# Two planes for the experts' rows, one engine for the normalised rows, and attention three items ahead

## The chip, the core and the metric

One core of a Trainium2 chip runs the whole program in one launch. Its engines are TensorE (PE, with PEld for the loading of its weights), VectorE (DVE), ScalarE (ACT), GpSimd (POOL) and SyncE (SP, which only issues DMAs here). The metric is the device time in microseconds; each time below is a median of several runs, beside one execution that was profiled.

## What is computed

Two blocks over 1024 tokens of width 1024, in float32. The first normalises, mixes (gated linear attention and causal pooling), adds, and then sends each token through two of 32 experts. The second has a short convolution and a dilated window attention, and adds again.

```python
def hier_moe(h, ...):                       # block 1, second half
    g_p, g_idx = lax.top_k(jax.nn.softmax(g_logits, axis=-1), 1)      # 1 of 4 groups
    e_top, e_idx = lax.top_k(e_logits, TOP_K_IN_GROUP)                # 2 of its 8 experts
    gate = g_p * jax.nn.softmax(e_top, axis=-1)
    ...                                     # rows sorted by expert, padded
    def expert_block(args):
        xb, e = args
        return (jax.nn.silu(xb @ w_gate[e]) * (xb @ w_up[e])) @ w_down[e]
    y_rows = y_rows * row_w[:, None]
    out = jnp.zeros((T + 1, D)).at[row_token].add(y_rows)[:T]

def first_block(x, ...):
    ...
    h2 = rmsnorm(x, norm2_g[l])
    x = x + hier_moe(h2, ...)
    return rmsnorm(x, norm_f_g)

def second_block(x, ...):
    h = rmsnorm_2(x, norm_w)
    u, g_b, g_c, z_conv, q, k, v, z_attn = jnp.split(h @ w_in, splits, axis=-1)
    y_conv = short_gated_conv(u, g_b, g_c, conv_w, conv_b) * jax.nn.silu(z_conv)
    for window, dilation in ((128, 1), (512, 4), (2048, 16)):
        o_i, lse_i = dilated_window_attention(q, k, v, rel_bias, window, dilation)
    o = softmax(lses) weighted sum of the o_i
    y = jnp.concatenate([y_conv, o * jax.nn.silu(z_attn)], axis=-1)
    return x + y @ w_out
```

## The kernel before

The tokens are eight tiles of 128 rows. Each float32 product is made of three matmuls: `split` (L124 to L131) casts an operand to its high part on ScalarE and subtracts that on VectorE for the low part (both stand as L127), and `mm3` (L160 to L163) multiplies high by high, high by low and low by high. Large tiles share a pool of slots named `blk`; an allocation waits for the last reader of the slot. Each engine and each DMA queue runs its instructions in one fixed order. SP's queue (q1 in the rows) carries the weights; POOL's queue (q0) carries the gathers, the scatters and some writes. A helper `late` holds closures back by a number of steps and so sets where small pieces of work stand between the matmuls.

**The router's end.** As a tile of block 1's first half is done, `route_rows` (L523) writes its x1 to the DRAM tensor `x_acc`, transposes it and splits it (`turn`), makes the router's logits and at last its normalised row h2, which goes to the DRAM tensor `h_rows`. Tiles 0 to 6 make h2 on VectorE (L568); tile 7 makes it with two multiplies on POOL (L531, L532), written by SP (L968). After the eighth tile `route_half`, `places` and `slots` give every token its row among its two experts' rows, by matmuls of one-hot tables (`val`, L653, and L664), and `row_tables` (L671 to L677) turns the sums into `row_idx`, the token of each of 96 rows of each expert, and `row_wgt`.

**The experts.** For each of 32 experts `gather_rows` (L980) fetches 96 rows of `h_rows` into one of four buffers `xg`, four experts ahead; `load_expert` (L270 to L285) loads six pieces of 512 KB of weights five experts ahead, a load waiting for the fifth before it; the rows are transposed, multiplied, and `down` scales the result into `yt` (L1045, ScalarE). `add_rows` (L985, POOL's queue) adds `yt` into `x_acc` by a scatter that accumulates. Unused rows have an index out of bounds and are skipped. The last expert's rows are added for tokens 0 to 511 by a matmul with one-hot `picks` straight into block 2's input (`add_last`, L1068 to L1076), since block 2 starts with them, and scattered too for the rest. A loop (`For_i`, L1128) for rows beyond 96 of an expert follows; here it runs no time, but every engine reads its bound behind its earlier work.

**Block 2's inputs.** After the loop `load_cols` (L308) loads x2 of tokens 0 to 511 as `x2c`, four loads of 512 KB. TensorE transposes them, and VectorE and ScalarE make the operands `g` (L129, L130). Tokens 512 to 1023 are loaded later by `load_x2` (L1219), while the products of the convolution run.

**The attention.** Four pairs of heads times twelve items (three dilations, four parts) make a stream of 48 items. For each, `load_values` loads `vt` from `v_rows` (three slots), `powers` multiplies queries and keys (L1500), takes a minimum on VectorE (L1506) and an exponential on ScalarE (L1508, into `sb`), `turn_powers` transposes `sb` (L1526) and copies it (L1528, L1530), and `weigh` multiplies with `vt` (L1559). The loop of L1684 runs `powers` two items ahead, `turn_powers` one ahead. `by_class` (L1480 to L1489) copies a pair's queries and keys into the order of a dilation, on POOL (L1487). `deliver` (L1655) loads partial sums `xs` by POOL's queue.

Of the kernel before, what the change touches and what calls it, by code (L numbers as in the profile page):

```python
# [20 lines left out]
P = 128  # L21
# [44 lines left out]
def first_then_second_block(ctx: ExitStack, tc: tile.TileContext, a: dict, out: bass.AP):  # L66
# [413 lines left out]
    row_idx = C.tile([P, NE], I32, name="row_idx")  # L480
    row_wgt = C.tile([P, NE], F32, name="row_wgt")
# [38 lines left out]
    last_h2 = []  # L520

    def route_rows(t, x1):
        ss = S.tile([P, 1], F32, name="ss1", tag="ss1", bufs=4)  # L523
        sq = blk("sq", (P, D))
        A.activation(sq, x1, AF.Square, accum_out=ss)
        r = mean_rstd(ss, 1, D)
        if t < NT - 1:
            G.dma_start(x_acc[t * P:(t + 1) * P], x1)  # L528
        else:
            h2 = blk("h2", (P, D))  # L530
            G.tensor_mul(h2, x1, r.to_broadcast([P, D]))  # L531
            G.tensor_mul(h2, h2, g2)  # L532
            G.dma_start(x_acc[t * P:(t + 1) * P], x1)
            last_h2.append(h2)
# [24 lines left out]

        def folded(lt):  # L560
            lp = psum((P, 36))
            PE.matmul(lp, lt, fold, start=True, stop=True)
            V.scalar_tensor_tensor(lgs[t // 4][:, t % 4, :], lp, r, br, op0=OP.mult, op1=OP.add)
            if t % 4 == 3:
                route_half(t // 4)
            if t < NT - 1:
# [21 lines left out]
    def route_half(hf):  # L588
# [26 lines left out]
        val = blk("val", (P, 4, 2, 5, NE), BF16)  # L615
        A.activation(val[:, :, :, 0, :], oh[:, ts], AF.Copy, scale=pcol)
        for i in range(4):
            A.activation(val[:, i, :, 1, :], oh[:, 4 * hf + i], AF.Copy, scale=float(4 * hf + i + 1))
        late.at(1 if hf else PLACES, lambda: places(hf, val, gp, e1, e2))

    def places(hf, val, gp, e1, e2):
# [31 lines left out]
        V.tensor_mul(val.rearrange("p t k v e -> p (t k) v e")[:, :, 2:, :],  # L653
# [4 lines left out]
    def slots(hf, val, sels):  # L658
        if hf == 0:
            slot_ps.append(psum((P, 5, NE)))  # L660
# [7 lines left out]
    def row_tables(idx, w, ps, n, pool):  # L668
        f = pool.tile([P, n], F32, name="ri_f", tag=f"rif{n}", bufs=1)
        e = pool.tile([P, n], F32, name="ri_e", tag=f"rie{n}", bufs=1)  # L670
        sv = pool.tile([P, 5, n], F32, name="ri_s", tag=f"ris{n}", bufs=1)  # L671
# [3 lines left out]
        V.scalar_tensor_tensor(idx, f, -float(P), e, op0=OP.add, op1=OP.add)  # L675
        V.tensor_add(e, sv[:, 2, :], sv[:, 3, :])
# [3 lines left out]
    def half(hf):  # L680
# [28 lines left out]
        if hf == 0:  # L709
            behind(lambda: w_q.extend(w_q0()))  # L710
        else:
            w_q += pair(w_in, 0)
        if hf == 0:
# [254 lines left out]
    SY.dma_start(h2_d[(NT - 1) * P:], last_h2[0])  # L968
    load_expert(3)
    late.flush()  # L970
    row_tables(row_idx, row_wgt, slot_ps[0], NE, R)
# [63 lines left out]
    def down(e):  # L1035
# [10 lines left out]
        if e < NE - 1:  # L1046
            add_rows(yt, row_idx[:, e:e + 1], CAP)
# [9 lines left out]
    last_idx = S.tile([P, 1], I32, name="last_idx", bufs=1)  # L1057
    picks = blk("picks", (P, 512), F32R)

    def place_last():  # L1060
        at = S.tile([P, 5], F32, name="last_at", bufs=1)
        V.tensor_copy(last_idx, row_idx[:, NE - 1:NE])
        V.tensor_copy(at[:, 4:], last_idx)
        for i in range(4):
            V.tensor_scalar(at[:, i:i + 1], at[:, 4:], float(-P * i), None, op0=OP.add)
            V.tensor_scalar(picks[:, i * P:(i + 1) * P], iota_s, at[:, i:i + 1], None, op0=OP.is_equal)

    def add_last(c):  # L1068
        for j in range(2):
            ps = psum((P, 2, 256))  # L1070
            for i in range(2):
                b = 2 * j + i
                for part in range(2):
                    PE.matmul(ps[:, i, :], picks[:CAP, b * P:(b + 1) * P], last_y[1 + part][:CAP, 256 * c:256 * c + 256],
# [51 lines left out]

    end_reg = nc.values_load(n_more[0:1, 0:1], min_val=0, max_val=NOB)
    with tc.For_i(0, end_reg, 1):  # L1128
# [24 lines left out]
        rv = E.tile([P, NT, 2, 5], BF16, name="rv")  # L1153
# [5 lines left out]
        sp = psum((P, 5))  # L1159
# [7 lines left out]
        row_tables(li, lw, sp.rearrange("p (a b) -> p a b", b=1), 1, E)  # L1167
# [36 lines left out]
        add_rows(lyt, li, P)  # L1204
# [10 lines left out]
    def load_x2():  # L1215
        xs = []
        for t in range(4, NT):
            xt = blk(f"x2_{t}", (P, D))
            SY.dma_start(xt, x_acc[t * P:(t + 1) * P])  # L1219
            xs.append(xt)  # L1220
# [52 lines left out]
    yc = [blk("yc0", (P, T))] + [W.tile([P, T], F32, name=f"yc{j}") for j in range(1, 4)]  # L1273
# [3 lines left out]
    qT = [blk(f"qT{j}", (P, T)) for j in range(4)]  # L1277
    for j in range(4):
        V.memset(qT[j][:, 0:1], 0.0)
        V.memset(kT[j][:, 0:1], 0.0)  # L1280
# [5 lines left out]
    def conv(hf, cc):  # L1286
# [35 lines left out]
        def convolve(m):  # L1322
            ct, u = 2 * cc + m, us[m]
            cv = yc[ct]
# [85 lines left out]
    for f in c0[:4] + c1[:4] + c0[4:] + c1[4:] + attn_gate(0):  # L1410
        f()
    x2 = load_x2()
# [167 lines left out]
    def mix_weights(hp):  # L1580
# [16 lines left out]
        def spread():  # L1597
            ps = psum((48, P))
            PE.transpose(ps, sw.rearrange("p c h b -> p (c h b)"), ident)
            swT = W.tile([48, P], F32, name="swT", tag="swT", bufs=1)  # L1600
# [84 lines left out]
    for g in range(-2, NS):  # L1685
        if g + 2 < NS:
            hp, cfg, pr = stream[g + 2]
            if g == -2:
# [89 lines left out]
```

## Time and profile before

| | us |
|---|---|
| median of 3 runs | 1626.17 (1624.89 to 1628.64) |
| the profiled execution | 1627.21 |
| its span (first to last instruction) | 1625.5 |
| busy in it: TensorE, VectorE, ScalarE, POOL | 1535.9, 1021.1, 801.2, 210.8 |

TensorE's mean granted clock is 0.972 of full speed. The experts take the stretch from about 640 to 985, the attention that from 1345 to 1570. Read busy times by stretch, not for the whole span; a stretch in which TensorE is busy throughout at clock 1.00 has nothing to gain from other engines. A wait names what came last before an instruction could start.

### The profile page before, as it was taken

What the parts mean: (1) busy time and instruction counts of PE and PEld (TensorE: products, weight loads), DVE (VectorE), ACT (ScalarE), POOL (GpSimd) and SP (SyncE); (2) the same over time, 40 slices, a digit from 0 to 9 for tenths busy, and PEclk for the clock granted to TensorE, in tenths of its full rate; (3) what the DMA queues carried; (4) which work ended last, traced back from release to release, by engine and by line L of the source; (5) the groups of instructions that cost most, each with busy time, mean ns of one, the idle gap of its engine ahead of it and who ended that gap; (6) DMA issues with size and microseconds to landing.
All of it is one profiled execution on the core that took longest, in us unless ns stands there. A gap on an engine that the chain in (4) does not pass through costs nothing. (4 is left out here: it accounts for less than half of the span.)

```text
span 1625.5 us, 24026 instructions
## 1 busy us (share of the span) xinstructions
PE 1535.9 (94%) x8678; PEld 1266.6 (78%) x8678; DVE 1021.1 (63%) x2278; ACT 801.2 (49%) x1635; POOL 210.8 (13%) x196
## 2 busy tenths in 40 slices
PE   7999999999999994999989897999999999999899
PEld 6888888887888874998888786888877787666667
DVE  5596444667644355998877686766655545676663
ACT  4434323453433232888777684524443326866550
POOL 1000000000000003232232111200000100243311
PEclk9999999999999996999999998999999999999999
DMA  6233334436323458999999996434423331445445
GB/s 193 65 82 106 103 109 163 136 115 195 104 80 115 142 215 281 295 270 319 328 312 335 296 335 194 156 102 164 149 88 104 104 103 41 120 119 147 103 137 169
DMA packets 168022, 272.01 MB, mean 167 GB/s; under 512 B 32689, under 2 KB 111932, under 8 KB 167773
## 3 DMA queue, kind: packets, MB, share of 16 engines
q1 hardware_dynamic: 154204, 232.13, 44.5%
q0 software_dynamic: 13680, 38.32, 8.5%
q8 instruction: 69, 1.13, 0.3%
q14 instruction: 53, 0.43, 0.1%
q10 hardware_dynamic: 16, 0.00, 0.0%
HBM read 243.92 MB, written 39.59 MB: 174 GB/s over the span
## 5 line engine op out<-in xcount | busy, mean ns | idle before, releaser
L127 ACT CAST wh<-wr 128x512 fp32r<-128x512 f32 (+1 forms) x248 | 170.6, 716 | 341.9 <-PE ps L162 192.5
L127 DVE TENSOR_TENSOR wl<-wr,wh 128x512 fp32r<-128x512 f32 (+1 forms) x248 | 202.3, 832 | 169.4 <-ACT wh L127 162.7
L127 DVE TENSOR_TENSOR wl<-ew,wh 128x1024 fp32r<-128x1024 f32 x144 | 172.6, 1220 | 44.3 <-ACT wh L127 43.6
L161 PE MATMUL ps<-h,wh 128*128 128x512 f32 x448 | 176.8, 395 | 0.0
L127 ACT CAST wh<-ew 128x1024 fp32r<-128x1024 f32 x144 | 149.7, 1052 | 54.4 <-PE ps L163 34.8
L163 PE MATMUL ps<-h,wl 128*128 128x512 f32 x448 | 175.3, 391 | 0.0
L162 PE MATMUL ps<-h,wh 128*128 128x512 f32 x448 | 175.3, 391 | 0.0
L161 PE MATMUL ps<-g,wh 128*128 128x512 f32 x320 | 126.1, 395 | 0.0
L162 PE MATMUL ps<-g,wh 128*128 128x512 f32 x320 | 125.2, 392 | 0.0
L163 PE MATMUL ps<-g,wl 128*128 128x512 f32 x320 | 124.8, 391 | 0.0
L161 PE MATMUL ps<-wh,xh 128*96 128x256 f32 x384 | 112.3, 293 | 6.2 <-ACT act L1023 6.2
L162 PE MATMUL ps<-wl,xh 128*96 128x256 f32 x384 | 110.9, 289 | 1.5 <-DVE wl L127 1.5
L163 PE MATMUL ps<-wh,xh 128*96 128x256 f32 x384 | 110.8, 289 | 0.0
L163 PEld LDWEIGHTS ps<-h,wl 128*128 128x128 f32 x448 | 84.6, 189 | 17.8
L161 PEld LDWEIGHTS ps<-h,wh 128*128 128x128 f32 x448 | 84.7, 189 | 17.5
L162 PEld LDWEIGHTS ps<-h,wh 128*128 128x128 f32 x448 | 84.6, 189 | 17.2
L985 POOL DMA_INDIRECT x_acc<-yt,row_idx x31 | 52.1, 1679 | 208.2 <-ACT yt L1045 147.6
L161 PE MATMUL ps<-wh,g 128*128 128x512 f32 x192 | 76.3, 398 | 0.0
L528 POOL DMA_DIRECT2D x_acc<-x x7 | 3.8, 536 | 551.7 <-DVE x L930 294.0
L163 PE MATMUL ps<-wh,g 128*128 128x512 f32 x192 | 75.1, 391 | 0.0
L162 PE MATMUL ps<-wl,g 128*128 128x512 f32 x192 | 74.9, 390 | 0.0
L161 PEld LDWEIGHTS ps<-wh,xh 128*96 128x96 f32 x384 | 65.8, 171 | 8.2 <-ACT act L1023 7.0
(455 smaller groups left out, 3642.0 us busy)
## 6 DMA issues: line engine op xcount, KB each, us to landing
wr<-in_w_in_dram SPq DMA_DIRECT2D x128, 512.0 KB, 3.9
ew<-in_w_exp_down_dram SPq DMA_DIRECT2D x64, 512.0 KB, 9.7
ew<-in_w_exp_gate_dram SPq DMA_DIRECT2D x64, 512.0 KB, 8.0
ew<-in_w_exp_up_dram SPq DMA_DIRECT2D x64, 512.0 KB, 9.5
wr<-in_w_out_dram SPq DMA_DIRECT2D x24, 512.0 KB, 3.9
xs<-xb_rows POOLq DMA_DIRECT2D x28, 256.0 KB, 3.3
x<-in_x_dram SPq DMA_DIRECT2D x12, 512.0 KB, 6.3
zb<-sw_d SPq DMA_DIRECT2D x24, 256.0 KB, 5.2
```

The source lines that it names most:

```text
L127: both = A.copy(hi, src), V.tensor_sub(lo, src, hi.bitcast(F32))
L161: PE.matmul(ps, lhs[0], rhs[0], start=start, stop=False)
L162: PE.matmul(ps, lhs[0], rhs[1], start=False, stop=False)
L163: PE.matmul(ps, lhs[1], rhs[0], start=False, stop=stop)
L528: G.dma_start(x_acc[t * P:(t + 1) * P], x1)
L985: G.indirect_dma_start(out=x_acc, out_offset=bass.IndirectOffsetOnAxis(ap=idx[:n], axis=0), in_=src[:n], in_offset=None, bounds_check=T - ...
```

## The change

1. `add_rows` becomes `put_rows`: a plain scatter into a new DRAM tensor `y_rows` of 2 x 1024 rows, where a row goes to token + 1024 k, k being 0 or 1 for a token's first or second expert. For this the one-hot tables carry a sixth value, k (two ScalarE instructions per half, 192 columns for 160 in the slot matmuls), and `row_tables` makes `row_place` besides `row_idx` (two small VectorE instructions more). The first 512 rows of each plane are zeroed by eight writes from a zeroed tile. `x_acc` then holds x1 alone, so the four loads of `x2c` are moved ahead of the loop; behind it eight loads of the planes' columns follow, which `add_last` adds on VectorE. `load_x2` loads two planes' rows to each tile and adds them: eight more loads and adds.
2. Tile 7's h2 is made by VectorE like the others and written by POOL's queue; tile 6's h2 is held back until tile 7 is transposed and split. In VectorE's order it stands behind that split, and tile 7's between the table `val` and the copy of the slot sums.
3. The attention runs `powers` and the loads three items ahead (`vt` gets a fourth slot), and the copies of `by_class` go to VectorE.

Tiles that are only needed later (`qT`, `yc0`, `picks`) are allocated later, and `swT` uses another pool.

```diff
-            G.tensor_mul(h2, x1, r.to_broadcast([P, D]))
-            G.tensor_mul(h2, h2, g2)
...
+            turned.add(t)
+            while unscaled:
+                unscaled.pop()()
...
+            def scaled_rows():
                 h2 = blk("h2", (P, D))
                 V.scalar_tensor_tensor(h2, x1, r, g2, op0=OP.mult, op1=OP.mult)
                 G.dma_start(h2_d[t * P:(t + 1) * P], h2)
+                if t == NT - 1:
+                    G.dma_start(x_acc[t * P:(t + 1) * P], x1)
+            if t == NT - 2 and NT - 1 not in turned:
+                unscaled.append(scaled_rows)
+            else:
+                scaled_rows()
...
-        val = blk("val", (P, 4, 2, 5, NE), BF16)
+        val = blk("val", (P, 4, 2, 6, NE), BF16)
+        for k in range(2):
+            A.activation(val[:, :, k, 5, :], oh[:, ts, k, :], AF.Copy, scale=float(k))
...
+        V.scalar_tensor_tensor(f, sv[:, 5, :], float(T), f, op0=OP.mult, op1=OP.add)
+        V.scalar_tensor_tensor(place, f, -float(P), e, op0=OP.add, op1=OP.add)
...
+            zero = blk("zero", (P, D))
+            G.memset(zero, 0.0)
+            for i in range(8):
+                r0_ = T * (i // 4) + P * (i % 4)
+                late.at(2 * i, lambda r0_=r0_: SY.dma_start(y_d[r0_:r0_ + P], zero))
...
-    SY.dma_start(h2_d[(NT - 1) * P:], last_h2[0])
...
-    def add_rows(src, idx, n):
-        G.indirect_dma_start(out=x_acc, out_offset=bass.IndirectOffsetOnAxis(ap=idx[:n], axis=0),
-                             in_=src[:n], in_offset=None, bounds_check=T - 1, oob_is_err=False, compute_op=OP.add)
+    def put_rows(src, place, n):
+        G.indirect_dma_start(out=y_d, out_offset=bass.IndirectOffsetOnAxis(ap=place[:n], axis=0),
+                             in_=src[:n], in_offset=None, bounds_check=2 * T - 1, oob_is_err=False)
...
     def add_last(c):
+        for y in yc2[c]:
+            V.tensor_add(xc2[c], xc2[c], y)
...
+    xc2, turn_part2 = load_cols(x_acc, "x2c")
     end_reg = nc.values_load(n_more[0:1, 0:1], min_val=0, max_val=NOB)
     with tc.For_i(0, end_reg, 1):
...
-    xc2, turn_part2 = load_cols(x_acc, "x2c")
-    add_rows(last_y[0], last_idx, CAP)
+    yc2 = []
+    for c in range(4):
+        yc2.append([])
+        for k in range(2):
+            yt = blk("y2c", (P, 4, 256))
+            SY.dma_start(yt, y_d[T * k:T * k + 512, 256 * c:256 * c + 256].rearrange("(i p) n -> p i n", p=P))
+            yc2[c].append(yt)
+    put_rows(last_y[0], last_place, CAP)
...
             SY.dma_start(xt, x_acc[t * P:(t + 1) * P])
+            for k in range(2):
+                yt = blk("y2", (P, D))
+                SY.dma_start(yt, y_d[T * k + t * P:T * k + (t + 1) * P])
+                V.tensor_add(xt, xt, yt)
...
-        v = hd[hp]["v"][cfg, pr] = W.tile([P, 3, P], F32, name="vt", tag="vt", bufs=3)
+        v = hd[hp]["v"][cfg, pr] = W.tile([P, 3, P], F32, name="vt", tag="vt", bufs=4)
...
-            G.tensor_copy(dst, src.rearrange("p (l r) -> p r l", r=n))
+            V.tensor_copy(dst, src.rearrange("p (l r) -> p r l", r=n))
...
-    for g in range(-2, NS):
-        if g + 2 < NS:
-            hp, cfg, pr = stream[g + 2]
+    LEAD = 3
+    for g in range(-LEAD, NS):
+        if g + LEAD < NS:
+            hp, cfg, pr = stream[g + LEAD]
```

SP's queue around the end of the loop for overflow rows (the branches). Before:

```order
L1128 UNCONDITIONAL_BRANCH
L308 DMA x2c_9871<-x_acc 128x4x256
L308 DMA x2c_9873<-x_acc 128x4x256
L308 DMA x2c_9875<-x_acc 128x4x256
L308 DMA x2c_9877<-x_acc 128x4x256
L1268 DMA gf<-in_norm_f_g_dram 128x1024
L116 DMA wr<-in_w_in_dram 128x4x256 x4
```

In the changed kernel, ahead of the loop:

```order
L116 DMA wr<-in_w_in_dram 128x4x256 x2
L308 DMA x2c_9690<-x_acc 128x4x256
L308 DMA x2c_9692<-x_acc 128x4x256
L308 DMA x2c_9694<-x_acc 128x4x256
L308 DMA x2c_9696<-x_acc 128x4x256
L1148 COMPARE_AND_BRANCH
```

and behind it (`y2c` are the columns of the two planes):

```order
L1148 UNCONDITIONAL_BRANCH
L1234 DMA y2c<-y_rows 128x4x256 x8
L1301 DMA gf<-in_norm_f_g_dram 128x1024
L116 DMA wr<-in_w_in_dram 128x4x256 x4
L1475 DMA b_12841<-skew 128x256 x2
```

The loads of `x2c` moved to the other side of the loop, and eight loads of the planes now stand ahead of `gf` and the weights.

VectorE behind the loop: the sums of `x2c` with the last expert's rows (from `ps`) and the first four operands `g`. Before:

```order
L127 TENSOR_TENSOR yhl<-yt,yhl 96x512
L1076 TENSOR_TENSOR x2c_9871<-x2c_9871,ps 128x512 x2
L1076 TENSOR_TENSOR x2c_9873<-x2c_9873,ps 128x512 x2
L1279 MEMSET qT_9909 128x1
L1279 MEMSET qT_9910 128x1
L1279 MEMSET qT_9911 128x1
L1279 MEMSET qT_9912 128x1
L130 SCALAR_TENSOR_TENSOR g_0_9892<-ps,gain_9888,g_0_9892 128x512
L130 SCALAR_TENSOR_TENSOR g_1_9893<-ps,gain_9888,g_1_9893 128x512
L130 SCALAR_TENSOR_TENSOR g_2_9894<-ps,gain_9888,g_2_9894 128x512
L130 SCALAR_TENSOR_TENSOR g_3_9895<-ps,gain_9888,g_3_9895 128x512
L1076 TENSOR_TENSOR x2c_9875<-x2c_9875,ps 128x512 x2
```

and in the changed kernel:

```order
L1087 TENSOR_TENSOR x2c_9690<-x2c_9690,y2c 128x1024 x2
L1095 TENSOR_TENSOR x2c_9690<-x2c_9690,ps 128x512 x2
L1087 TENSOR_TENSOR x2c_9692<-x2c_9692,y2c 128x1024 x2
L1087 TENSOR_TENSOR x2c_9694<-x2c_9694,y2c 128x1024
L1095 TENSOR_TENSOR x2c_9692<-x2c_9692,ps 128x512 x2
L1087 TENSOR_TENSOR x2c_9694<-x2c_9694,y2c 128x1024
L130 SCALAR_TENSOR_TENSOR g_0_9930<-ps,gain_9926,g_0_9930 128x512
L130 SCALAR_TENSOR_TENSOR g_1_9931<-ps,gain_9926,g_1_9931 128x512
L130 SCALAR_TENSOR_TENSOR g_2_9932<-ps,gain_9926,g_2_9932 128x512
L130 SCALAR_TENSOR_TENSOR g_3_9933<-ps,gain_9926,g_3_9933 128x512
L1095 TENSOR_TENSOR x2c_9694<-x2c_9694,ps 128x512 x2
L1087 TENSOR_TENSOR x2c_9696<-x2c_9696,y2c 128x1024
```

The adds of the planes, for the third columns too, stand ahead of the first `g`; the last split `yhl` has gone ahead of the loop.

TensorE in the attention, where the third dilation begins: its powers are 128x128, its transposes come in fours, those of the second dilation in sixes. Before:

```order
L1500 MATMUL ps<-kd,qd 128x128 x4
L1526 MATMUL ps<-ident,sb 128x128 x6
L1559 MATMUL ps<-pt,vt 64x128 x8
L1500 MATMUL ps<-kd,qd 128x128 x4
L1526 MATMUL ps<-ident,sb 128x128 x4
```

and in the changed kernel:

```order
L1535 MATMUL ps<-kd,qd 128x128 x4
L1561 MATMUL ps<-ident,sb 128x128 x6
L1594 MATMUL ps<-pt,vt 64x128 x8
L1535 MATMUL ps<-kd,qd 128x128 x4
L1561 MATMUL ps<-ident,sb 128x128 x6
L1594 MATMUL ps<-pt,vt 64x128 x8
L1535 MATMUL ps<-kd,qd 128x128 x4
L1561 MATMUL ps<-ident,sb 128x128 x4
```

Between the first powers of the dilation and their transposes one other item's powers stood before; now there are two.

## Rows read from the trace of the kernel before

**Rows 1.** The page, engine table: busy us (share of the span), instructions

```profile
PE 1535.9 (94%) x8678; PEld 1266.6 (78%) x8678; DVE 1021.1 (63%) x2278; ACT 801.2 (49%) x1635; POOL 210.8 (13%) x196
```

**Rows 2.** Stages: stretch, us, engines busy (instructions), clock, DMA share, GB/s

```profile
614.00:660.00 46.00, 24.55 (x189) 22.44 (x190) 27.44 (x85) 17.71 (x30) 16.61 (x15) 0.67 0.84 273
660.00:760.00 100.00, 100.00 (x744) 91.01 (x743) 91.94 (x126) 88.14 (x125) 29.47 (x20) 1.00 0.95 298
760.00:940.00 180.00, 157.82 (x1071) 141.57 (x1070) 131.87 (x156) 128.19 (x186) 42.50 (x30) 0.94 0.97 318
...
985.00:1010.00 25.00, 16.46 (x77) 13.69 (x76) 10.11 (x20) 7.01 (x12) 2.83 (x2) 0.73 0.74 219
...
1060.00:1150.00 90.00, 90.00 (x399) 74.55 (x398) 53.19 (x101) 33.08 (x52) 4.36 (x8) 1.00 0.47 160
...
1345.00:1570.00 225.00, 207.95 (x1609) 150.52 (x1608) 141.57 (x536) 151.08 (x538) 58.00 (x46) 0.96 0.42 113
```

**Rows 3.** DMA queues, 660 to 980: kind, packets, MB, share of 16 engines

```profile
q1 hardware_dynamic: 23686, 84.53, 75.4%
q0 software_dynamic: 6065, 14.59, 20.3%
```

**Rows 4.** DMA, 988 to 993, one adding scatter almost alone

```profile
q0 software_dynamic: 112, 0.29, 39.3%
```

**Rows 5.** DMA, 636 to 640, gathers

```profile
q0 software_dynamic: 143, 0.23, 21.9%
```

**Rows 6.** DMA, 1133 to 1142, plain writes; then KB each, us to landing

```profile
q0 software_dynamic: 636, 2.33, 66.3%
...
xb_rows<-u POOLq DMA_DIRECT2D x4, 512.0 KB, 3.8
```

**Rows 7.** Waits, 660 to 980: engine, tile, line <- releaser: us, times, longest

```profile
POOL x_acc L985 <- DMA x_acc<-yt,row_idx: 38.5, 7, 8.4
...
ACT ehl L127 <- DMA ew<-in_w_exp_up_dram: 13.2, 4, 7.2
```

**Rows 8.** Busy time, 311 to 324, where the added zeroing would lie

```profile
311.00:324.00 13.00, 13.00 (x81) 9.95 (x81) 8.66 (x25) 4.20 (x9) 1.06 (x2) 1.00 0.50 172
```

**Rows 9.** VectorE's timeline, router's end: start, us, instruction, [idle before <- releaser]

```profile
617.90 1.28 DVE L568 SCALAR_TENSOR_TENSOR h<-x,rsq_y,g 128x1024 f32<-128x1024 f32 x1
...
633.43 0.32 DVE L672 COPY ri_s<-ps 128x160 f32<-128x160 f32 x1 [1.34 <-PE ps L664]
```

**Rows 10.** POOL's timeline, the first gather

```profile
635.18 1.06 POOL L980 DMA_INDIRECT xg<-h_rows,row_idx  x1 [7.67 <-DVE last_at L1065]
```

**Rows 11.** Chain of waits, end of block 1: start, us, what

```profile
987.26 5.24 DMA x_acc<-yt,row_idx
...
993.31 3.50 DMA x2c<-x_acc
```

**Rows 12.** VectorE's timeline at the second load of x2

```profile
1130.63 1.22 DVE L127 TENSOR_TENSOR wl<-wr,wh 128x1024 fp32r<-128x1024 f32 x1 [0.18 <-ACT wh L127]
```

**Rows 13.** VectorE's timeline, start of block 2

```profile
996.90 1.28 DVE L1076 TENSOR_TENSOR x2c<-x2c,ps 128x512 f32<-128x512 f32 x2 [2.10 <-DMA x2c<-x_acc]
...
1013.90 1.40 DVE L130 SCALAR_TENSOR_TENSOR g<-ps,gain,g 128x512 fp32r<-128x512 f32 x2
```

**Rows 14.** Waits, attention, 1345 to 1570

```profile
PE ps L1526 <- ACT sb L1508: 9.1, 8, 2.7
...
PE ps L1559 <- DMA vt<-v_rows: 6.3, 3, 2.7
```

**Rows 15.** VectorE's timeline beside a pair of POOL's copies

```profile
1503.36 0.69 DVE L1530 COPY pt<-ps 128x512 f32<-128x512 f32 x1
1503.96 4.95 DVE L127 TENSOR_TENSOR wl<-wr,wh 128x1024 fp32r<-128x1024 f32 x1
```

**Rows 16.** POOL's timeline, one pair of copies by class

```profile
1503.78 2.08 POOL L1487 COPY qd<-qT 128x1024 f32<-128x1024 f32 x1
1505.80 2.02 POOL L1487 COPY kd<-kT 128x1024 f32<-128x1024 f32 x1
```

More of the change, by code (lines that the diff above doesn't have):

```diff
@@ L517, in first_then_second_block @@
     lgs = {}
-    last_h2 = []
+    turned, unscaled = set(), []
     def route_rows(t, x1):
@@ L659, in slots @@
         if hf == 0:
-            slot_ps.append(psum((P, 5, NE)))
+            slot_ps.append(psum((P, 6, NE)))
         for i in range(4):
@@ L666, in slots, with row_tables @@
                           start=t == 0 and k == 0, stop=t == NT - 1 and k == 1)
-    def row_tables(idx, w, ps, n, pool):
+    def row_tables(idx, place, w, ps, n, pool):
         f = pool.tile([P, n], F32, name="ri_f", tag=f"rif{n}", bufs=1)
         e = pool.tile([P, n], F32, name="ri_e", tag=f"rie{n}", bufs=1)
-        sv = pool.tile([P, 5, n], F32, name="ri_s", tag=f"ris{n}", bufs=1)
+        sv = pool.tile([P, 6, n], F32, name="ri_s", tag=f"ris{n}", bufs=1)
         V.tensor_copy(sv, ps)
@@ L967, in first_then_second_block @@
     load_expert(2)
-    SY.dma_start(h2_d[(NT - 1) * P:], last_h2[0])
     load_expert(3)
     late.flush()
-    row_tables(row_idx, row_wgt, slot_ps[0], NE, R)
+    row_place = extra[0].tile([P, NE], I32, name="row_place")
+    row_tables(row_idx, row_place, row_wgt, slot_ps[0], NE, R)
     wg, wu, wd = w_experts
@@ L1056, in first_then_second_block @@
     last_y = []
-    last_idx = S.tile([P, 1], I32, name="last_idx", bufs=1)
-    picks = blk("picks", (P, 512), F32R)
+    last_place = E.tile([P, 1], I32, name="last_place")
+    picks = []
     def place_last():
-        at = S.tile([P, 5], F32, name="last_at", bufs=1)
-        V.tensor_copy(last_idx, row_idx[:, NE - 1:NE])
-        V.tensor_copy(at[:, 4:], last_idx)
+        at = E.tile([P, 5], F32, name="last_at")
+        picks.append(blk("picks", (P, 512), F32R))
+        V.tensor_copy(last_place, row_place[:, NE - 1:NE])
+        V.tensor_copy(at[:, 4:], row_idx[:, NE - 1:NE])
         for i in range(4):
             V.tensor_scalar(at[:, i:i + 1], at[:, 4:], float(-P * i), None, op0=OP.add)
-            V.tensor_scalar(picks[:, i * P:(i + 1) * P], iota_s, at[:, i:i + 1], None, op0=OP.is_equal)
+            V.tensor_scalar(picks[0][:, i * P:(i + 1) * P], iota_s, at[:, i:i + 1], None, op0=OP.is_equal)
     def add_last(c):
+        for y in yc2[c]:
+            V.tensor_add(xc2[c], xc2[c], y)
         for j in range(2):
@@ L1073, in add_last @@
                 for part in range(2):
-                    PE.matmul(ps[:, i, :], picks[:CAP, b * P:(b + 1) * P], last_y[1 + part][:CAP, 256 * c:256 * c + 256],
+                    PE.matmul(ps[:, i, :], picks[0][:CAP, b * P:(b + 1) * P], last_y[1 + part][:CAP, 256 * c:256 * c + 256],
                               start=part == 0, stop=part == 1)
@@ L1152, in first_then_second_block @@
         V.tensor_reduce(mark.rearrange("p t k -> p (t k)"), hit, axis=AX.X, op=OP.add)
-        rv = E.tile([P, NT, 2, 5], BF16, name="rv")
+        rv = E.tile([P, NT, 2, 6], BF16, name="rv")
         V.tensor_scalar(rv[:, :, :, 0], mark, pcol, None, op0=OP.mult)
@@ L1166, in first_then_second_block @@
         lw = E.tile([P, 1], F32, name="lw")
-        row_tables(li, lw, sp.rearrange("p (a b) -> p a b", b=1), 1, E)
+        lp = E.tile([P, 1], I32, name="lp")
+        row_tables(li, lp, lw, sp.rearrange("p (a b) -> p a b", b=1), 1, E)
         gather_rows(xg[0], li, P)
@@ L1219, in load_x2 @@
             SY.dma_start(xt, x_acc[t * P:(t + 1) * P])
+            for k in range(2):
+                yt = blk("y2", (P, D))
+                SY.dma_start(yt, y_d[T * k + t * P:T * k + (t + 1) * P])
+                V.tensor_add(xt, xt, yt)
             xs.append(xt)
@@ L1272, in first_then_second_block @@
     w_in2 = a["w_in_2"]
-    yc = [blk("yc0", (P, T))] + [W.tile([P, T], F32, name=f"yc{j}") for j in range(1, 4)]
+    yc = [None] + [W.tile([P, T], F32, name=f"yc{j}") for j in range(1, 4)]
     edge = W.tile([P, 4, 2], F32, name="edge")
@@ L1276, in first_then_second_block @@
     kT = [B.tile([P, T], F32, name=f"kT{j}", tag="wb", bufs=4) for j in range(4)]
[L1277 to L1280, printed above, removed]
     v_d = tc.dram_tile([T, 512], F32, name="v_rows")
@@ L1323, in convolve @@
             ct, u = 2 * cc + m, us[m]
+            if yc[ct] is None:
+                yc[ct] = blk("yc0", (P, T))
             cv = yc[ct]
@@ L1411, in first_then_second_block @@
         f()
+    qT = [blk(f"qT{j}", (P, T)) for j in range(4)]
+    for j in range(4):
+        V.memset(qT[j][:, 0:1], 0.0)
+        V.memset(kT[j][:, 0:1], 0.0)
     x2 = load_x2()
@@ L1599, in spread @@
             PE.transpose(ps, sw.rearrange("p c h b -> p (c h b)"), ident)
-            swT = W.tile([48, P], F32, name="swT", tag="swT", bufs=1)
+            swT = W.tile([P, 512], F32, name="swT", tag="tmp", bufs=NTMP)[:48, :P]
             A.copy(swT, ps)
```

18 lines of the change are left out of this document (8 added, 10 removed).

## The prediction

> **What bounds the kernel now.** I read the page's engine table first, then busy time by stage, then in each stage that the change touches the waits, the transfers and single instructions. TensorE is busy for 94% of the span [rows 1]; a change pays only where TensorE stands idle or runs at its lower clock, and those places differ by stage [rows 2]. From 660 to 760 it is busy for 100.00 of 100 us. From 760 to 940, still in the expert loop, for 157.82 of 180, with a DMA share of 0.97. From 614 to 660, the router in front of the experts, for 24.55 of 46 at clock 0.67. From 985 to 1010, where block 1 ends, for 16.46 of 25 at 0.73. From 1060 to 1150, where the second load of x2 lies, for all 90.00. In the attention, 1345 to 1570, for 207.95 of 225 at 0.96.
>
> **Experts: plain scatter in place of adding scatter.** In this stage the weights' queue has 75.4% of the time of the 16 DMA engines and the POOL queue (gathers and scatters) 20.3% [rows 3]. With all engines full from 760 on, time taken off the POOL queue lets weights come sooner. Its 20.3% of 320 us is 65.0 us for 14.59 MB, in 29 scatters and 25 gathers, so 0.27 MB each. A scatter almost alone moved 0.29 MB in 39.3% of 5 us, 1.97 us, so 148 GB/s [rows 4]; gathers at the loop's start moved 0.23 MB in 21.9% of 4 us, 0.88 us, so 263 GB/s [rows 5]. At those rates 29 scatters and 25 gathers cost 29 x 1.82 + 25 x 1.03 = 78.6 us; the stage shows 65.0, so I scale by 0.83: 1.51 and 0.85 us each. No row of before shows a plain scatter. It moves whole 4 KB rows as a gather does, so I price it as one: 0.66 us saved each. By the plain writes of this queue later on (2.33 MB in 66.3% of 9 us, 390 GB/s, [rows 6]) it would be 0.57 us and save 0.94. If its price is mostly per row it saves perhaps 0.2. Some 26 scatters lie ahead of the last weights: 17, 24 or 5 us of DMA time. The cap is TensorE's own pace: 22.2 us idle from 760 to 940 and 6% of its clock there [rows 2], some 30 us. I take **-14**, a little below the middle, since part of the idle time is a wait for slots (range -24 to -2). The 38.5 us in which POOL waited for an earlier scatter [rows 7] are not added: the new scatters still go into one DRAM tensor and wait for each other, and behind them on POOL stand only gathers that run four experts ahead. The waits for weights that ScalarE shows, of which the 13.2 us are the largest [rows 7], are what should shrink.
>
> **Zeroing.** One memset on POOL and eight 512 KB writes on SP's queue, in a stretch with TensorE busy for 13.00 of 13 us and a DMA share of 0.50 [rows 8]. Eight writes at 350 GB/s (84.53 MB in 75.4% of 320 us, [rows 3]) are 12 us of the queue, and the weights behind them are loaded several ahead: **0** (0 to +2; if the cover were gone, 12).
>
> **Router's end.** Tile 6's row (1.28 us, [rows 9]) stood on VectorE ahead of the low halves of tile 7's split, which the logits wait for; it goes behind them: -1.1. Tile 7's row goes from two POOL multiplies and an early write on SP's queue to one VectorE instruction, for which I take the same 1.28, between the last value table and the copy of the row table at 633.43, where VectorE idles 1.34 us [rows 9]. But its write is now the last before the first gather, which left at 635.18 [rows 10]. Issued at about 632.4 with the 3.8 us that a 512 KB write of this queue took [rows 6], it lands near 636.5, so the gather leaves some 1.5 us later, and with it the first transposes; behind it on POOL wait the other three gathers. Two more small VectorE steps and 32 more columns in eight matmuls: below 0.5. **+1.5** (-1 to +3).
>
> **End of block 1.** The loop for overflow rows makes all engines wait for the earlier work, and the last loop scatter was issued at 987.26 and landed 5.24 later; then x2c was loaded, 3.50 from 993.31 [rows 11]. With cheaper scatters the last ones no longer queue up, and x2c is loaded ahead of the loop. What then ends last is the split of the last expert's rows, near 990: -2.7. Against this stand eight loads of 0.52 MB behind the loop, 1.5 us each at 350 GB/s, so the last lands some 15 us in (3.5 + 8 x 1.5), and eight adds of 128x1024. A VectorE instruction of that shape with two inputs takes 1.22 [rows 12]: 9.8 us, in the order of VectorE ahead of the casts g that TensorE needs. Before, x2c's sums ran from 996.90 and the last g ended at 1015.30 [rows 13], with VectorE busy for 10.11 of the 25 us to 1010 [rows 2]. So about half of the 9.8 falls into gaps: +5.1. The gf and weight loads queued behind the y loads on SP come 12 us later, which I find covered by the g chain. Sum **+2.4** (-2 to +8, the upper end with TensorE longer at its lower clock, 0.73 in the mean here).
>
> **Second load of x2.** Eight more loads and adds: 4.2 MB, 12 us of the queue, and 9.8 us of VectorE, between 1110 and 1150. The query weights' split stands at 1130.63 [rows 12], while TensorE is never idle [rows 2]; the weights queued behind these loads on SP have several splits' lead. The chain would end some 10 us later, near 1149, and I estimate that it is needed near 1152. **0** (0 to +4; if the lead is gone, 10).
>
> **Attention.** TensorE waits here 9.1 us, in 8 pieces, the longest 2.7, for ScalarE's exp before the transposes, and 6.3 us, longest 2.7, for values [rows 14]. An item takes 225/48 = 4.7 us. Being three items ahead gives each exp and each value load one item more, above the longest of these waits. So up to 15.4 us go, at most the 17.05 of idle time and the 4% of clock on 208 us, 8. What is late next: the output weights and the copies pt, which the change doesn't move; I leave a third to them. The copies by class move from POOL to VectorE, 12 of 16 in this stretch. A PSUM copy of half the size took 0.69 there [rows 15], so 1.38 each, 16.6 us on an engine busy for 141.57 of 225 [rows 2]: 70% of it used, while POOL took 2.08 and 2.02 for a pair [rows 16]. A pair, 2.8 us, stands in front of the next reductions, exps and copies pt; the item gained covers it. **-11** (-18 to +5). One split took 4.95 us, against 1.22 elsewhere [rows 12, 15], just while POOL ran such a pair [rows 16]; that excess of 3.7 us, seen once at this size, should go.
>
> The Trainium skill ("SBUF — State Buffer", section "SBUF: two separate sides") says that VectorE instructions with two SBUF inputs and a POOL instruction that reads SBUF lock each other out for a whole instruction; the long split agrees. The same section says that a float32 copy from SBUF to SBUF on VectorE keeps POOL from writing its DMAs' descriptors, which speaks against moving the copies; no row here shows it. By the first alone the sum stays; what the second would do is rival B.
>
> **The rivals.**
> A. *The experts are not held by DMA time*: the weights wait for slots or a fixed latency, or the plain scatter costs as much as the adding one, since it still goes row by row and one behind the other. For: loads are paced five in flight. Against: a share of 0.97 [rows 2]. Experts 0: -7, **1619**.
> B. *The copies eat the attention's gain*: on VectorE, in order, each pair delays reductions and holds up POOL's loads of xs. If all 16.6 us of copies add to what I take, -11 becomes +5.6: -4.5, **1622**; with the half of it 1613. For: VectorE's reductions and the exps behind them are what TensorE waits for. Against: VectorE has 83 us free there.
> C. *Slower: the planes are paid where they are read.* 16 loads (24 us) and 16 adds (19.5 us) stand in front of x2 in both places; if neither hides, because VectorE takes them in order and the weights queue behind them, 43.5 us come, in place of the 5.1 that I count. Without them the sum is -14 + 1.5 - 2.7 - 11 = -26.2, so it turns slower from 26 us on, 60% of it; with all of it +17, **1643**. For: TensorE already idles at the block's end. Against: TensorE has matmuls for all the 90 us around the second load [rows 2].
>
> **How the numbers follow.** -14 + 1.5 + 0 + 2.4 + 0 - 11 = -21.1. The profiled execution took 1627.21 (span 1625.5 and 1.7 around it), so 1606.1; the median of the three runs is 1.0 lower: **1605**. Chances: this forecast, 1594 to 1613, 0.57; A 0.17; B 0.14; C, in whole or part, 0.12. About 0.2%, 3.3 us, is what a measurement can tell from no change. Faster by more: forecast, A and most of B, 0.85. Within: 0.06, out of B and C. Slower: 0.09. The range takes in A and B and the experts' upper bound with the rest as forecast: 1592 to 1622.
>
> **What would show it.** Right: POOL queue's share from 660 to 980 near 15%, TensorE's idle time from 760 to 940 down by 10 us or more; first gather 1 to 2 us after its place relative to the router's start; the last g some 28 us after the loop; in the attention the waits for exp and values almost gone and no split near 5 us. Wrong: expert idle time as before (A); VectorE's reductions late by a pair of copies (B); TensorE idle between 1060 and 1150 or 30 us and more after the loop (C).

## The result

| | before | changed |
|---|---|---|
| median, us | 1626.02 (1624.89 to 1628.64, 4 runs) | 1599.72 (1598.62 to 1604.49, 4 runs) |
| ratio, 95% interval | | 0.9842 (0.9819 to 0.9865) |
| profiled execution, its span, us | 1627.21, 1625.5 | 1598.6, 1596.9 |
| TensorE's mean granted clock | 0.972 | 0.976 |

The forecast was 1605 (1592 to 1622), a gain of 21; the gain came out at 26. A second comparison on another chip gave a ratio of 0.9835 (0.9810 to 0.9861).

The page of the changed kernel (engine table):

```profile
PE 1518.2 (95%) x8678; PEld 1258.5 (79%) x8678; DVE 1042.5 (65%) x2313; ACT 801.5 (50%) x1639; POOL 161.9 (10%) x180
```

Busy time by stage in the changed kernel, columns as in [rows 2]:

```profile
660.00:760.00 100.00, 100.00 (x743) 90.96 (x743) 92.31 (x129) 87.50 (x125) 24.20 (x20) 1.00 0.94 320
760.00:940.00 180.00, 166.74 (x1190) 151.37 (x1189) 146.22 (x175) 144.43 (x207) 39.81 (x33) 0.97 0.97 337
...
985.00:1010.00 25.00, 21.17 (x97) 17.50 (x98) 20.96 (x26) 10.24 (x27) 0.91 (x1) 0.76 0.86 271
1060.00:1150.00 90.00, 90.00 (x405) 74.55 (x404) 58.18 (x108) 33.04 (x52) 4.32 (x8) 1.00 0.59 212
1340.00:1570.00 230.00, 223.87 (x1721) 168.27 (x1720) 159.86 (x573) 154.70 (x545) 40.09 (x45) 0.99 0.46 126
```

Against [rows 2], TensorE is busy for 9 us more from 760 to 940 and stays busy through the second load of x2. In the attention it is idle for 6 of 230 us in place of 17 of 225, and its clock is 0.99 in place of 0.96.

The span became 28.6 us shorter. To see where, the same instructions are compared in both profiles, each shift counted from the one before. Tile 7's transposes start at 614.50 before and at 616.04 after, so **+1.5**. This comes from the first 40 us, which the change doesn't touch: TensorE waits there 5.2 us for VectorE's first scales in place of 3.5. The first scaling of an expert's result comes at 666.3 and 670.6, so **+2.7** more. The expert loop runs from the first scaling to the last:

```profile
L1045 ACT ACTIVATE yt<-ps,row_wgt x64: 666/677/711, 666.3 to 987.8; 96x512 f32<-96x512 f32 x64
```

```profile
L1061 ACT ACTIVATE yt<-ps,row_wgt x64: 667/676/721, 670.6 to 974.4; 96x512 f32<-96x512 f32 x64
```

The first fence is the line that scales the results in the kernel before, the second is the same line in the changed one; "666.3 to 987.8" are its first and last start in us. The loop's 321.5 us became 303.8, **-17.7**. From the last scaling to the end of the last operand g of block 2 it took 27.5 us (987.8 to 1015.3, [rows 13]) and now takes 32.6 (974.4 to 1007.0), **+5.1**. From there to the first powers of the attention, at 1353.2 and 1345.6, the shift is **+0.7**. From the first powers to the end of the span 272.3 us became 251.3, **-21.0**. The sum is -28.7. Two profiles of the changed kernel differ by 3.2 us in their spans and by 4.5 in the loop, so the shifts up to the loop's end are no sharper than that.

### The profile page after: what moved, and what is told of

Same layout as the page of the kernel before. It is cut to its first block, busy times and chain, and to the rows that moved or that the text cites. A ratio compares the mean times of both kernels' runs of the same rounds, so it can differ in the third digit from the quotient of the medians.

```text
span 1596.9 us, 24024 instructions
## 1 busy us (share of the span) xinstructions
PE 1518.2 (95%) x8678; PEld 1258.5 (79%) x8678; DVE 1042.5 (65%) x2313; ACT 801.5 (50%) x1639; POOL 161.9 (10%) x180
## 5 line engine op out<-in xcount | busy, mean ns | idle before, releaser
L127 DVE TENSOR_TENSOR wl<-wr,wh 128x512 fp32r<-128x512 f32 (+1 forms) x248 | 195.7, 806 | 158.7 <-ACT wh L127 156.2
L161 PEld LDWEIGHTS ps<-h,wh 128*128 128x128 f32 x448 | 84.7, 189 | 17.7
L161 PEld LDWEIGHTS ps<-g,wh 128*128 128x128 f32 x320 | 60.5, 189 | 13.0 <-issue 0.6
L163 PEld LDWEIGHTS ps<-g,wl 128*128 128x128 f32 x320 | 60.4, 189 | 12.5
L162 PEld LDWEIGHTS ps<-g,wh 128*128 128x128 f32 x320 | 60.4, 189 | 12.3 <-DVE g L130 0.2
```

Of the source, the lines that this page charges most:

```text
L127: both = A.copy(hi, src), V.tensor_sub(lo, src, hi.bitcast(F32))
L161: PE.matmul(ps, lhs[0], rhs[0], start=start, stop=False)
L162: PE.matmul(ps, lhs[0], rhs[1], start=False, stop=False)
L163: PE.matmul(ps, lhs[1], rhs[0], start=False, stop=stop)
```

## The experiments

The kernels ran in three groups, each on one chip, and each was compared with the kernel before on its chip, whose median was 1629.0, 1627.3 and 1627.8 us. Times of different groups are therefore compared by their ratios.

**1. One part at a time.** The third part alone on the kernel before (the look-ahead, the fourth slot, `swT` in another pool, the copies on VectorE):

```diff
-name="vt", tag="vt", bufs=3)
+name="vt", tag="vt", bufs=4)
...
-            G.tensor_copy(dst, src.rearrange("p (l r) -> p r l", r=n))
+            V.tensor_copy(dst, src.rearrange("p (l r) -> p r l", r=n))
...
-    for g in range(-2, NS):
...
+    LEAD = 3
+    for g in range(-LEAD, NS):
```

> The kernel before with the third part alone: powers and loads of values three items ahead, four slots for values, copies by class on VectorE. In the changed kernel the time from the first powers to the end fell by some 21 us against before. If that is the work of this part alone, about 1626 - 21 = 1605 us. Rival: part of it came from the other parts (other slots of the shared pool, transfers moved in time), then 1610 us or more.

Measured 1606.38 us, ratio 0.9857 (0.9823 to 0.9890). From the first powers to the end its profile has 251.0 us, as the changed kernel has (251.3). So the attention's gain is the work of this part alone.

The first part alone: the changed kernel with the other two undone.

```diff
+            G.tensor_mul(h2, x1, r.to_broadcast([P, D]))
+            G.tensor_mul(h2, h2, g2)
...
-            V.tensor_copy(dst, src.rearrange("p (l r) -> p r l", r=n))
+            G.tensor_copy(dst, src.rearrange("p (l r) -> p r l", r=n))
...
-    LEAD = 3
-    for g in range(-LEAD, NS):
...
+    for g in range(-2, NS):
```

> The changed kernel with the second and third parts undone: plain scatter, planes, zeroing, earlier x2c. In the changed kernel the first to the 31st expert's result took 298.7 us against 316.3 before (-17.6), and the end of block 1 cost 2 us more. If these belong to the first part alone: -14 to -17, 1609 to 1612 us. Rival: the expert loop was shortened because it began later and found more weights loaded; then -8 or less, 1618 or more.

Measured 1625.18 us, ratio 0.9982 (0.9960 to 1.0004): a miss, and by its number on the rival's side. But the rival's reason, a later start of the loop, doesn't hold either: with a start 2.4 us later than before the loop took 308.4 us (668.7 to 977.1), 13 less. Of these 13, 9.6 are lost elsewhere in this profile: 2.4 ahead of the first result, 5.5 at the end of block 1, 0.4 and 1.3 from there on. For this part the prediction's steps sum to -14 + 2.4 = -11.6. It is worth about 3 us (by its interval between a gain of 6.5 and a loss of 0.7). Nearly the whole result is thus the third part's: 0.9857 x 0.9982 = 0.9839.

**2. What holds the expert loop.** The kernel before with rows written in place of added, which leaves the experts' sum out and only prices the scatter:

```diff
-                             in_=src[:n], in_offset=None, bounds_check=T - 1, oob_is_err=False, compute_op=OP.add)
+                             in_=src[:n], in_offset=None, bounds_check=T - 1, oob_is_err=False)
```

> The kernel before with the accumulation of its scatters taken out: rows are written over those of x_acc and not added, so the experts' sum is left out; nothing else moves. It prices the plain scatter without planes. If the adding scatter's DMA time was the cost, the loop shortens by about 17 us and the scatters' tail at the end of block 1 with it: 1604 to 1610 us. Rival, that the gain came from something else in the change: within 5 us of before, 1621 or more.

Measured 1609.43 us, ratio 0.9886 (0.9858 to 0.9914). Its loop runs 301.1 us, and no plane has to be read back:

```profile
L1045 ACT ACTIVATE yt<-ps,row_wgt x64: 662/677/708, 667.3 to 968.4; 96x512 f32<-96x512 f32 x64
```

So the plain scatter by itself is worth about 18 us, and what the planes bring with them gives most of it back. The opposite test has each scatter made twice in the changed kernel, the second time into a tensor that nobody reads:

```diff
     def put_rows(src, place, n):
         G.indirect_dma_start(out=y_d, ...)
+        G.indirect_dma_start(out=y2_d, ...)
```

> The changed kernel with each expert's rows scattered a second time into a tensor that nobody reads: 0.27 MB more per expert on POOL's queue. If the loop is held by the time of the DMA engines, 26 scatters at about 0.66 to 0.85 us each come back: +15 to +25 us, 1615 to 1625. Rival, that the loop now runs at TensorE's pace or waits for slots: under +5 us, 1605 or less.

Measured 1617.02 us, ratio 0.9927 (0.9907 to 0.9948). That is some 14 us above the changed kernel by the ratios (0.9842), a little under what was expected, and far from the rival's 5. Its loop and its busy time from 760 to 940:

```profile
L1064 ACT ACTIVATE yt<-ps,row_wgt x64: 668/677/712, 669.6 to 997.2; 96x512 f32<-96x512 f32 x64
```

```profile
760.00:940.00 180.00, 159.77 (x1073) 142.91 (x1072) 130.55 (x151) 127.49 (x181) 58.21 (x45) 0.92 0.96 339
```

The loop takes 327.5 us: more transfers on POOL's queue bring the idle time back. Over all kernels the loop took 319.6 to 321.5 us with adding scatters (four of them, in the mean 320.4), 303.5 to 310.5 with plain ones (eight, 306.5), and 301.1 and 327.5 in these two. The DMA queues from 660 to 960, in the changed kernel:

```profile
q1 hardware_dynamic: 23706, 84.90, 80.6%
q0 software_dynamic: 6048, 14.41, 15.0%
```

POOL's queue needs 15.0% of 300 us, 45 us, for what took 65.0 before [rows 3]. The 20 us taken off and the 17.7 that the loop lost belong together: the loop is held by the time of the DMA engines.

Another reading would be that scatters delay the loop by their place in POOL's order, with the gathers late behind them. The waits speak against it. From 760 to 940 TensorE's list of waits has none for a gathered tile, and ScalarE's waits for weights follow the scatters. In the changed kernel they are

```profile
ACT wh L127 <- DMA ew<-in_w_exp_up_dram: 9.2, 7, 3.0
ACT ehl L127 <- DMA ew<-in_w_exp_up_dram: 7.1, 3, 5.5
ACT wh L127 <- DMA ew<-in_w_exp_gate_dram: 3.5, 3, 2.5
```

which is 19.8 us. The same waits sum to 28.3 us before, to 14.0 without adding, and to 34.5 with each scatter made twice.

**3. The attention taken apart.** The diff of the third part above without its `tensor_copy` lines, and these lines alone:

> As the run with the third part alone, but the copies by class stay on POOL: only the look-ahead and the fourth slot. If TensorE's waits for exp and values (15.4 us) carry the gain, 1608 to 1612 us, and a split of about 5 us beside a pair of copies is still there. Rival: the copies on POOL hold VectorE up and carry half of the gain, then 1615 us or more.

> The kernel before with the copies by class on VectorE alone, look-ahead two as before. If only the long splits beside POOL's copies go, -2 to -5 us: 1621 to 1624. Rival, that the copies stand in VectorE's way without the item gained: slower than 1628. Rival, that they carry half of the gain: 1616 or less.

Measured 1621.18 us, 0.9944 (0.9928 to 0.9960), and 1622.91 us, 0.9970 (0.9949 to 0.9991). The first is outside my theory, which had put the gain on the look-ahead, and on the side of its rival; the second is inside. From the first powers to the end their profiles have 266.2 and 265.6 us, so each alone gives 6 to 7 and both together 21. From the first powers to the last product, with the look-ahead alone and with the copies alone (columns as in [rows 2]):

```profile
1353.70:1559.20 205.50, 191.65 (x1555) 141.57 (x1556) 126.95 (x519) 142.56 (x525) 56.73 (x46) 0.96 0.44 120
```

```profile
1350.30:1555.00 204.70, 192.90 (x1554) 139.02 (x1555) 142.91 (x533) 143.34 (x524) 34.37 (x33) 0.97 0.44 122
```

TensorE is idle there for 13.9 and 11.8 us, in place of 16.1 before and 5.0 in the changed kernel, and its clock is 0.96 and 0.97, in place of 0.96 and 0.99 (the rows of these two stand in the next section). TensorE's waits in the attention, with the look-ahead alone:

```profile
PE ps L1559 <- ACT pt L1528: 7.6, 3, 4.0
PE ps L1526 <- DVE xs L1656: 2.2, 2, 2.0
PE ps L1526 <- ACT og L1561: 1.9, 1, 1.9
```

with the copies alone:

```profile
PE ps L1526 <- ACT sb L1508: 4.8, 7, 1.2
PE ps L1559 <- DMA vt<-v_rows: 4.3, 2, 2.3
```

and in the changed kernel:

```profile
PE ps L1594 <- ACT pt L1563: 4.0, 2, 2.6
PE ps L1594 <- DVE pt L1565: 1.1, 3, 0.4
```

The look-ahead takes both waits of [rows 14] away, and others come in their place. The longest is for the copy `pt`, made on ScalarE behind the split of an output weight. ScalarE's wait for those weights with the look-ahead alone, and in the run with the whole third part:

```profile
ACT wh L127 <- DMA wr<-in_w_out_dram: 11.4, 3, 4.9
```

```profile
ACT wh L127 <- DMA wr<-in_w_out_dram: 3.8, 1, 3.8
```

With the copies on VectorE as well two of the three are gone. Why the weights come in time in one order and not in the other wasn't tried and stays open. The copies themselves shorten the waits of [rows 14] from 15.4 to 9.1 us; on VectorE a pair takes

```profile
1442.38 1.10 DVE L1487 COPY qd<-qT 128x1024 f32<-128x1024 f32 x1
1443.39 1.10 DVE L1487 COPY kd<-kT 128x1024 f32<-128x1024 f32 x1
```

a little over half of POOL's time [rows 16].

No split took 5 us with the look-ahead alone, though POOL kept its copies (1.22 or 1.23 each). That it was a split that became long in [rows 15] was chance. The stretching itself is not: other VectorE instructions show it. A multiply of 128x512, which closes a pair of heads, takes (shortest, median and longest in ns) with the look-ahead alone, with the copies alone and with both:

```profile
L1617 DVE TENSOR_TENSOR og<-og,zb x6: 680/1272/2506, 1431.6 to 1532.6; 128x512 f32<-128x512 f32 x6
```

```profile
L1617 DVE TENSOR_TENSOR og<-og,zb x6: 1332/1750/1772, 1427.9 to 1527.7; 128x512 f32<-128x512 f32 x6
```

```profile
L1617 DVE TENSOR_TENSOR og<-og,zb x10: 680/686/693, 1431.3 to 1555.1; 128x512 f32<-128x512 f32 x10
```

The longest, 2.5 us at 1482.16, runs beside POOL's copy of 1481.63 to 1484.11. With the copies alone these multiplies run beside POOL's own work on `og` (1424.45 to 1433.74 in the first pair of heads), and with both beside neither. How much of the 21 us this carries isn't separated.

**4. The router's end.** The changed kernel with the second part undone, and with tile 7's row alone back on POOL and SP (the diff; the first also takes out the holding back of tile 6's row):

```diff
+        else:
+            h2 = blk("h2", (P, D))
+            G.tensor_mul(h2, x1, r.to_broadcast([P, D]))
+            G.tensor_mul(h2, h2, g2)
+            G.dma_start(x_acc[t * P:(t + 1) * P], x1)
+            last_h2.append(h2)
...
-            else:
+            elif t < NT - 1:
                 scaled_rows()
...
     load_expert(2)
+    SY.dma_start(h2_d[(NT - 1) * P:], last_h2[0])
     load_expert(3)
```

> The changed kernel with the second part undone: tile 7's normalised row made by two multiplies on POOL and written by SP's queue between the third and fourth expert's loads, tile 6's row ahead of tile 7's split. In the changed kernel the first gather left 6.4 us later than before, 1.2 of them older than the router. If that is the late write of tile 7's row: 4 to 6 us faster than the changed kernel, 1594 to 1596. Rival, that the later start is given back in the loop (weights already loaded): same, 1598 to 1601.

> As the run before, but tile 6's row stays behind tile 7's split as in the change; only tile 7's row goes back to POOL and SP. If the logits' earlier start of about 1.1 us reaches the gathers: 1 us faster than the run with the whole part undone, 1593 to 1595. Rival, that POOL's multiplies then hold VectorE's chain up and eat it: 1595 or more.

Measured 1601.36 us, 0.9838 (0.9819 to 0.9858), and 1599.38, 0.9815 (0.9792 to 0.9838). The first is the rival's case: no difference from the changed kernel. The second lies on its rival's side (1595 or more). POOL's timeline in the changed kernel (last write of a row, clearing of two gather buffers, first gather):

```profile
633.04 0.53 POOL L568 DMA_DIRECT2D h_rows<-h  x1 [10.03 <-DVE h L567]
633.56 1.86 POOL L993 MEMSET xg<- 128x1024 f32 x2
641.54 1.05 POOL L996 DMA_INDIRECT xg<-h_rows,row_idx  x1 [6.12 <-issue]
```

The gather leaves 25.5 us behind tile 7's transposes; before it was 20.7 ([rows 10], 614.50). Of these 4.8 us, 2.7 are left at the first result. Because two clearings stand behind the write, I put them in front of it:

```diff
+    xg = [blk(f"xg{i}", (P, D)) for i in range(FA + 1)]
+    for t in xg:
+        G.memset(t, 0.0)
     load_expert(2)
     load_expert(3)
     late.flush()
...
-    xg = [blk(f"xg{i}", (P, D)) for i in range(FA + 1)]
-    for t in xg:
-        G.memset(t, 0.0)
```

> The changed kernel with the four clearings of the gather buffers on POOL ahead of the write of tile 7's row instead of two ahead and two behind. If the clearings behind it held its transfer up and slowed VectorE's small steps beside them (1.96 and 1.87 us in place of 0.18), the first gather comes 3 to 4 us earlier behind tile 7's transposes, 22 us, and those steps are short. Rival, that the write is slow because the weights' queue is full: the gather as late as before, 25 us.

Measured 1598.83 us, ratio 0.9838 (0.9805 to 0.9870), beside

> The changed kernel itself, beside the three that follow on the same chip: 0.984 of before, about 1600 us where before takes 1626. It serves as the base for their differences.

which gave 1600.91, 0.9835 (0.9810 to 0.9861): the same time. In the rows the step is clear. POOL with the clearings in front:

```profile
621.37 1.86 POOL L985 MEMSET xg<- 128x1024 f32 x2
633.27 0.53 POOL L568 DMA_DIRECT2D h_rows<-h  x1 [10.04 <-DVE h L567]
637.97 1.05 POOL L996 DMA_INDIRECT xg<-h_rows,row_idx  x1 [4.17 <-issue]
```

From the write to the gather it takes 4.7 us in place of 8.5, and the gather leaves 21.7 behind the transposes (637.97 against 616.25). VectorE's step on the table of rows in the changed kernel, and here:

```profile
633.50 1.96 DVE L681 TENSOR_SCALAR ri_e<-ri_s 128x32 f32<-128x32 f32 x1
```

```profile
633.73 0.18 DVE L681 TENSOR_SCALAR ri_e<-ri_s 128x32 f32<-128x32 f32 x1
```

The small VectorE instruction lasts until both of POOL's clearings (0.97 us each) are over. The Trainium skill ("SBUF — State Buffer", section "SBUF: two separate sides") says that the two engines share a pair of ports that one of them holds for a whole instruction. These two rows agree that VectorE waits; it waited here for two instructions, not for one. Whether the write was slow because of the clearings alone isn't separated: from 633 to 636 the weights' queue had 64.3% of the engines in the changed kernel and 4.4% here.

The kernel with tile 7's row back on POOL was run again beside the changed one:

> The changed kernel with tile 7's normalised row back on POOL's multiplies and SP's queue, as before. In one profile each, the first gather stood 25.5 us behind tile 7's transposes in the changed kernel, 20.7 before, some 21 here. If this reaches the end, 2 to 4 us below the changed kernel beside it; rival, that the loop gives it back since weights go on loading meanwhile: within 1.5 us of it.

Measured 1596.80 us, 0.9822 (0.9795 to 0.9849), against 0.9835; by the ratios that is 2 us, the lower edge of what was expected. Both times it is below the changed kernel, by 0.27 and 0.13%, and both times the intervals overlap: a better version isn't shown.

**5. The end of block 1.** The changed kernel without the eight adds of planes to the first 512 tokens, which leaves the experts' rows out there and only prices the adds:

```diff
     def add_last(c):
-        for y in yc2[c]:
-            V.tensor_add(xc2[c], xc2[c], y)
         for j in range(2):
```

> The changed kernel without the eight adds of the two planes to the first 512 tokens' x2 (this leaves the experts' rows out there); the loads stay. From the 31st expert's result to the end of block 2's last operand g the changed kernel took 37.7 us, before 32.6. If the adds in VectorE's order are the cost: 31 to 33 us, total 4 to 6 below the changed kernel. Rival, that the loads and the scatters in front of the loop are: still 36 us or more.

Measured 1597.89 us, ratio 0.9824 (0.9794 to 0.9854). From the last scaling (975.9) to the last g (1008.6) it takes 32.7 us, as with the adds (32.6). The rival's forecast holds: the adds are not what costs. ScalarE's timeline there without the adds, and with them:

```profile
999.45 0.62 ACT L127 CAST wh<-wr 128x512 fp32r<-128x512 f32 x1 [10.11 <-DMA wr<-in_w_in_dram]
```

```profile
996.38 0.62 ACT L127 CAST wh<-wr 128x512 fp32r<-128x512 f32 x1 [2.13 <-DMA wr<-in_w_in_dram]
```

Without the adds ScalarE stands idle for 10.11 us before the first weights, which wait on SP's queue behind the planes' loads. The weights come 23.5 us behind the last scaling here and 22.0 with the adds. Two chains of about the same length run side by side, the adds and those weights, and taking one away gives nothing. That taking both away would give something wasn't tried.

## Why the prediction held, and where it didn't

- **Experts, -14 forecast.** The loop lost 17.7 us in the changed kernel, and 13.9 in the mean over the kernels with plain scatters (320.4 to 306.5). The step was right, and so was its price by a gather's (0.66 us each); POOL's share of 15% came as written. TensorE's idle time from 760 to 940 fell from 22.2 to 13.3 us, 8.9 in place of the 10 that I had named as the sign. Rival A is out by both tests of the second experiment.
- **Zeroing, 0.** This was right: from 312 to 330, where the eight writes lie, TensorE is busy for 18.00 of 18 us in both kernels.
- **Router's end, +1.5.** The gather came 4.8 us later, above the range's +3, and the first result 2.7. VectorE's part came out better than forecast: its copy of the row table stands 17.1 us behind tile 7's transposes (633.11) in place of 18.9 [rows 9]. The write took all of that back and more: it needed 8.5 us up to the gather, not 3.8 to its landing. I had priced it by a write of another stage, and had not looked at what stands behind it on POOL. It doesn't show in the total, as the first run of the fourth experiment says. That the loop gives it back, because weights go on loading meanwhile, is likely and not shown.
- **End of block 1, +2.4.** It measured +5.1, inside its range. The step that failed first is "the last ones no longer queue up". The chain of the changed kernel there:

```profile
965.80 7.64 DMA y_rows<-yt,row_place
...
974.21 3.79 DMA y_rows<-yt,row_place
...
980.71 8.36 DMA y2c<-y_rows
```

  The last scatter but one of the loop took 7.64 us to land, longer than the 5.24 of [rows 11], and the last one waited for it. The four loads of x2c were issued beside it, at 963.78; that they made it slow isn't shown. So the scatter still ended last, and landed 3.6 us behind the last scaling in place of 4.7: 1.1 us won where I had counted 2.7. The stretch from the first sum on VectorE to the last g grew by 6.4 us (18.4 to 24.8) where I had counted 5.1 for the adds. The weights that I had called covered were covered only by the adds, as the fifth experiment shows.
- **Second load of x2, 0.** TensorE is busy for 90.00 of 90 us again, and the stretch to the attention grew by 0.7. Rival C is out there. How much lead was left isn't known: the 1149 and 1152 of the prediction rest on no row shown, and no run tried them.
- **Attention, -11.** It measured -21, beyond the -18 of its range; this is the term that was mis-sized. TensorE from the first powers to the last product, before and after:

```profile
1353.20:1564.70 211.50, 195.37 (x1556) 140.93 (x1555) 132.52 (x519) 143.60 (x524) 57.46 (x45) 0.96 0.44 118
```

```profile
1345.60:1536.20 190.60, 185.56 (x1557) 137.87 (x1556) 133.29 (x533) 142.62 (x525) 30.75 (x33) 0.99 0.48 130
```

  Idle time fell from 16.1 to 5.0 us, which is the 11 that I took. But the same matmuls also needed 9.8 us less, 195.37 to 185.56, while the mean granted clock rose from 0.96 to 0.99. Before, parts of the stretch ran at the lower of the two levels, 1.2 GHz in place of 2.4, one of them behind 1 us in which TensorE had nothing to do (1438 to 1439):

```profile
1440.00:1446.00 6.00, 6.00 (x26) 3.87 (x26) 2.58 (x14) 3.91 (x17) 4.33 (x3) 0.50 0.55 132
```

  By these means the clock took 4% of 211.5 us before and 1% of 190.6 after, so it accounts for some 6.6 of the 9.8 us; the rest isn't taken apart. I named 8 us for the clock as part of the cap and left them out of the value. Rival B is out, since the copies alone gained. Out is also my reading that the look-ahead does it and the copies cost: each alone takes 2 to 4 us of idle time, and it takes both for the 11.
- **The sum.** The nearness of 21 and 26 is partly luck. It hides two errors that cancel in part: the planes give back more of the scatter's gain than I counted, and the attention gains twice as much. In the one profile above, the shifts from the first result to the attention sum to -9.2 us (2.7 - 17.7 + 5.1 + 0.7), in place of the 3 by which the medians tell the first part's worth; its loop of 303.8 us is one of the shortest of the eight.

## What to carry to other kernels

Where a stage is held by the DMA engines' time, price each transfer in engine time by a row of its own kind, and take off what the new layout must read back later: here some 18 us of cheaper scatters became about 3. TensorE's stalls showed up twice here, as idle time and as matmuls at a lower granted clock; count both when waits are removed. And before two changes are judged one by one, look which wait each of them leaves standing: here the halves gave 0.6 and 0.3%, and both together 1.4%.

## What was not expected of the hardware

- VectorE's instruction on 32 columns lasted 1.96 us beside two clearings on POOL, and 0.18 without them. A multiply of 128x512 took 0.68 to 2.51 us, the longest beside one of POOL's copies.
- A float32 copy of 128x1024 with strided reads took 1.10 us on VectorE, 2.08 on POOL [rows 16]; I had expected 1.38 on VectorE, as worked out from a copy out of PSUM.
- The loop's last two scatters landed in 7.64 and 3.79 us, and the expert loop of kernels with plain scatters varied between 303.5 and 310.5 us from profile to profile.
